# The second bias on the weights' queue, and the last expert's transposes ahead of its second product

## The chip, the cores and the metric

The kernel runs on one core of one Trainium2 chip. The metric is device microseconds of one launch, the median of the runs shown. A profile of one execution gives its span, from the first to the last instruction, and the busy time of each engine: TensorE (PE; its weight loads apart as PEld), VectorE (DVE), ScalarE (ACT), GpSimd (POOL) and the queue processor SyncE (SP). Transfers run on 16 DMA engines; they are issued here from SyncE's queue and from ScalarE's.

## The reference

One decoder layer on 256 tokens of width 1024, all in float32: a mixer (pooling, sparse attention and forgetting attention, merged by gates), a layer norm, then a mixture of experts and a second layer norm. The change lies in the mixture of experts. Cut to what matters:

```python
logits = xf @ router_w + router_b              # 256 tokens, 32 experts
top_v, top_i = lax.top_k(logits, 4)
gates = jax.nn.softmax(top_v, axis=-1)
# for every expert e and its tokens:
h = xblk @ w1[e] + b1[e]                       # 1024 -> 2048
gate, upv = jnp.split(h, 2, axis=-1)
gate = jnp.minimum(gate, 7.0); upv = jnp.clip(upv, -7.0, 7.0)
act = (upv + 1.0) * (gate * jax.nn.sigmoid(1.702 * gate))
y_e = act @ w2[e] + b2[e]                      # 1024 -> 1024
# y = sum over a token's experts of its gate times y_e
x = layer_norm(ALPHA * x + y, ln2_g, ln2_b)
```

`moe_b2`, the second bias, is a table of 32 experts by 1024 numbers, 128 KB. Its part of the result is the gates, 256 x 32, times this table.

## The kernel before

The mixer fills the first quarter of the span. The experts then run one after the other in a loop over `e` from 0 to 30, with expert 31 written out behind it. Each expert has 64 slots for tokens; where an expert has more, a second pass handles them (`overflow`, not taken here). An expert reads 12 MB of weights: four tiles of 2 MB for its first product (`First(e).load()`, a quarter of the 1024 rows each) and two for its second (`Second(e).load()`). Its steps are `gemm1` (64 slots by 1024 by 2048, into the two banks `h`), copies to `hs` by ScalarE and VectorE, `act` (transposes by TensorE, then bias, clamps, sigmoid and products on VectorE and ScalarE, into `a_main`), `gemm2` (into the bank `u`), and `scatter`, which spreads the slots over the tokens and adds them in the four banks `acc`. The second product of an expert runs within the pass of the next one; so pass `e` loads the first weights of `e` and then the second weights of `e - 1`.

All weights are issued by SyncE in one written order (`in_order`). They go into a ring of 11 places of 2 MB, by turns, so that a load can be issued when TensorE has read the load that stood 11 places earlier. Each transfer also signals on one of eight semaphores, which the order's rows name DMAHW0 to DMAHW7. They are given out in turn over the transfers of both queues, and a transfer is issued only when the one that had its semaphore before has landed.

The second bias was loaded in pass 2 by `load_biases`, with two transfers of 64 KB on ScalarE's queue, into `xg[2]`, a buffer for gathered tokens that is free for that time (the trace names it `rws`). In pass 3 `gated_biases` multiplies it with the gates into `acc`. Later, in pass 29, `norm_rows` puts the gain and the bias of the second layer norm as rows into a buffer `gb2` of its own pool.

Expert 31 is written out to the end. Its first product is taken with the first half of the columns finished first (`c` = 0), so that the activation of that half runs beside the product's other half. `act(..., c, DVE, parts=n)` handles half `c`: four transposes on TensorE, then the elementwise steps in `n` pieces. Its second product takes eight slices `j` of 128 rows: slices 0 to 3 need the activation's first half, 4 to 7 the second. Slices 0 to 5 run over all columns, 6 and 7 over one half of the columns at a time, so that the copy, the last `scatter` and the norm's sums of the first half start early. Its weights are loaded by `Last().load()`: slices 0 to 3 as 2 MB, slices 4 and 5 as 1 MB, slices 6 and 7 as two column halves of 512 KB.

Instructions issued through `PE`, `DVE`, `ACT` or `GPS` keep the order in which they are written; their line in the profile is line 48, the helper's.

Of the kernel before, what the change touches and what calls it, by code (L numbers as in the profile page):

```python
# [9 lines left out]
F32 = mybir.dt.float32  # L10
# [11 lines left out]
E = 32  # L22
# [29 lines left out]
def hybrid(ctx: ExitStack, tc: tile.TileContext, A, out, dbg=None):  # L52
    nc = tc.nc
    PE, DVE, ACT = Pinned(tc, nc.tensor), Pinned(tc, nc.vector), Pinned(tc, nc.scalar)
    GPS = Pinned(tc, nc.gpsimd)
    A = {n: a[0] for n, a in A.items()}
# [61 lines left out]
    b1T = consts.tile([128, 16, E], F32, name="b1T")  # L118
# [28 lines left out]
    def mm_tile(cols=256):  # L147
        return ps.tile([128, 512], F32, name="mm", bufs=3)[:, :cols]
# [17 lines left out]
    rows = mp.tile([128, 128], F32, name="rows")  # L166
# [96 lines left out]
    for t in range(2):  # L263
        for h in range(2):
            warm0(WARM_X[t * 2 + h])
            p = mm_tile(512)
# [3 lines left out]
            r = (slice(None), kq[h], slice(t * 128, (t + 1) * 128))  # L270
# [18 lines left out]
    def fm(w, c0, parts=None, pe=None, p=None, copy=nc.vector.tensor_copy):  # L289

        hi, lo = parts or hi_lo(8)
        if not parts:
            split(hi, lo, w[:, :, c0:c0 + 128], copy)
        if p is None:
            p = mm_tile(256)
        if pe:
            for n, (a, b) in enumerate(((hi, xh), (hi, xl), (lo, xh))):
                for k in range(8):
                    pe.matmul(p, a[:, k], b[:, k], start=(n == k == 0), stop=(n == 2 and k == 7))
        else:  # L300
            for k in range(8):
                mm3(p, (hi[:, k], lo[:, k]), (xh[:, k], xl[:, k]), k == 0, k == 7)
        return p
# [34 lines left out]
    for i in range(2):  # L338
        p = cmp_p[i]
# [24 lines left out]
    for br in range(2):  # L364
        p = fm(None, 0, kd_parts[br])
# [15 lines left out]
    p = mm_tile(256)[:32, :]  # L381
# [8 lines left out]
    p = mm_tile(64)  # L390
# [26 lines left out]
    for c in range(2):  # L417
        w = win((512 + 256 * c, 768 + 256 * c))
        for i in range(2):
            p = fm(w, i * 128)  # L420
            nc.scalar.activation(qn[:, 2 * c + i, :], p, AF.Identity, bias=col(R_A + 4 + 2 * c + i), scale=1.0)

    p = mm_tile(256)
# [461 lines left out]
    def slots(src, ts, dve=nc.vector):  # L885

        n = src.shape[-1]
        sh = [128, ts.stop - ts.start, n, SLOTS]
        return dve.tensor_tensor(S[:, ts, :n], src.unsqueeze(3).to_broadcast(sh),
                                 iota_s[:, None, None, :].to_broadcast(sh), op=OP.is_equal).ins  # L890

    def row_set(v, j, n):

        return v[:, j // n * n * 128:(j // n + 1) * n * 128].rearrange("p (c r) -> p r c", r=n)[:, j % n]
# [45 lines left out]
    norm_row_pool = ctx.enter_context(tc.tile_pool(name="norm_rows", bufs=1, side="right", reuse_waits="tile"))  # L940
    rings['x'] = xp
    r = turn[0] % len(order)
# [7 lines left out]
    def u_tile():  # L950
        return ps.tile([128, 512], F32, name="u", bufs=2)
# [4 lines left out]
    def h_tile(c):  # L956
        return ps.tile([128, 512], F32, name=f"h{c}")
# [36 lines left out]
    xg = [t2[:, b * 512:(b + 1) * 512].rearrange("p (k s) -> p k s", k=8) for b in range(2)]  # L994
# [41 lines left out]
    a_main = t2[:, 1024:1536].rearrange("p (j s) -> p j s", j=8)  # L1036
# [42 lines left out]
    def weigh(gsrc, x):  # L1079

        for t in range(2):
            nc.gpsimd.tensor_tensor(SG[:, t], S[:, t, x:x + 1].to_broadcast([128, 2, SLOTS]),  # L1082
                                    gsrc[:, t].unsqueeze(2).to_broadcast([128, 2, SLOTS]), op=OP.mult)

    def weigh_last(gsrc):

        for x in range(2):
            nc.gpsimd.tensor_tensor(S[:, :, x], S[:, :, 1], gsrc.to_broadcast([128, 2, SLOTS]), op=OP.mult)
# [9 lines left out]
    def gemm1(xg, w1):  # L1098

        hp = [h_tile(c) for c in range(2)]  # L1100
        for k in range(8):
            for c in range(2):
                for half in range(2):
                    PE.matmul(hp[c][half * 64:(half + 1) * 64], xg[:, k],
                              w1(k, half * 2 + c), start=(k == 0), stop=(k == 7), skip_group_check=True)
        nc.scalar.copy(hs[:, :512], hp[0])  # L1106
        nc.vector.tensor_copy(hs[:, 512:], hp[1])  # L1107
# [24 lines left out]
    def in_order(w, src):  # L1132
        return tc.keep_in_program_order(nc.sync.dma_start(w, src))

    def First(e):
        return Rows(w1v, e)

    def Second(e):
        return Rows(w2v, e)
# [64 lines left out]
    def act(*args, **kw):  # L1204
        for _ in act_steps(*args, **kw):
            pass
        return args[1]
# [14 lines left out]
                                 start=first, stop=False,  # L1222
                                 skip_group_check=True)

    def load_biases(dst):

        for h in range(2):
            ACT.dma_start(dst[h * E:(h + 1) * E], A['moe_b2'][:, h * 512:(h + 1) * 512])

    def gated_biases(b2r):  # L1230
        GT = lp.tile([128, T], F32, name="GT")
# [41 lines left out]

    def norm_rows():

        gb2 = norm_row_pool.tile([128, 2048], F32, name="gb2").rearrange("p (r c) -> p r c", c=128)
        for q in range(4):
            p = u_tile()
            for j in range(4):
                r = q * 4 + j  # L1280
                nc.tensor.matmul(p[:, j * 128:(j + 1) * 128], ident[:16, r:r + 1].to_broadcast([16, 128]), rows2,
                                 start=(j == 0), stop=(j == 3), skip_group_check=True)
            nc.scalar.copy(gb2[:, q * 4:(q + 1) * 4], p.rearrange("p (j c) -> p j c", j=4))
        return [gb2[:, i * 8:(i + 1) * 8].rearrange("p r c -> p (r c)") for i in range(2)]

    def gates(e):
        return G[:, :, e:e + 1]
# [5 lines left out]
    for e in range(E - 1):  # L1293
        buf, odd = e % 2, e % 2 == 1
        if e == E - 3:
            g2, b2 = norm_rows()
        w1 = First(e).load()
        if 0 < e < E - 2:
            w2 = Second(e - 1).load()
        if e:  # L1300
            weigh(gates(e), buf)
            if e == E - 2:
                weigh_last(gates(E - 1))
            if odd:
                slots(rk[:, :, e + 1:e + 3], slice(0, 2))
        gemm1(xg[e % 3], w1)
        if e == 0:
            p = u_tile()
            for c in range(4):
                PE.transpose(p[:, c * 128:(c + 1) * 128], row_set(b1r, c, 4), ident)  # L1310
            nc.scalar.copy(b1T.rearrange("p (q c) e -> p c q e", q=4), p.rearrange("p (c q e) -> p c q e", c=4, q=4))
            with tc.issue_after(last_pe), tc.issue_after(last_act), tc.issue_after(last_dve):
                acc[1] = [acc_tile(1, h) for h in range(2)]
                gates_and_counts()
            weigh(gates(0), 0)
            gT = turn_slots(0, u_tile())
            a = act(b1T[:, :, e], a_main)
        elif e < E - 2:
            if late:
                scatter(*late)  # L1320
                late = None
            a = xg[e % 3] if e == E - 3 else a_main
            steps = act_steps(b1T[:, :, e], a, banks=[u_tile(), h_tile(0)])
            next(steps)
            if e == 3:
                gated_biases(b2r)
            if odd:
                find(e + 1, 0, h_tile(1))
            else:
                gT = turn_slots(buf, h_tile(1))  # L1330
            gemm2(prev[0], w2)
            for _ in steps:
                pass
            if odd:
                gT = turn_slots(buf, h_tile(0))
                find(e + 1, 1, u_tile())
            late = prev[1], e == 1
            if e == 2:
                b2r = xg[2].rearrange("p k s -> p (k s)")
                load_biases(b2r)  # L1340
            if e == SUMS:
                scatter(*late)
                late = None
                residuals()
            if e == E - 3:

                scatter(*late)
                gemm2(a, Second(e).load())
        else:
            gT = turn_slots(buf, u_tile())  # L1350
            a = a_main
            steps = [act_steps(b1T[:, :, e], a, c, DVE) for c in range(2)]
            for c in range(2):
                next(steps[c])
            scatter(prev[1])
            gTn = turn_slots(1 - buf, h_tile(0), S)
            for c in range(2):
                for _ in steps[c]:
                    pass
            w2 = Second(e).load()  # L1360
            last = Last().load()
            gemm2(a, w2)
        prev = (a, gT)
# [9 lines left out]
    for c in range(2):  # L1373
        for k in (6, 7):
            last.first(banks, k, c)
        nc.scalar.copy(hs[:, c * 512:(c + 1) * 512], banks[c])
        if c:
            yp = h_tile(0)
            for j in (0, 1):
                last.second(yp, j, slice(0, 512))  # L1380
        act(b1T[:, :, E - 1], a_main, c, DVE, parts=2 - c)
    for j in range(2, 6):
        last.second(yp, j, slice(0, 512))

    def row_sums():
# [8 lines left out]
    for c in range(2):  # L1394
# [4 lines left out]
        for t in range(2):  # L1399
            for h in range(2):  # L1400
                r = slice(h * 64, (h + 1) * 64)
# [56 lines left out]
```

## Time and profile before

| | before |
|---|---|
| median of 3 runs (lowest, highest) | 1199.18 us (1198.42, 1199.37) |
| the profiled execution, its own time | 1200.99 us |
| its span | 1199.1 us |
| TensorE busy | 1128.9 us, 94% |
| VectorE busy | 347.7 us, 29% |
| ScalarE busy | 208.8 us, 17% |
| DMA, mean over the span | 375 GB/s |
| mean granted TensorE clock | 0.995 |

The span is cut in 40 slices of 30 us where the page shows rates over time. Busy shares are means over stages with different limits: the mixer (to about 260 us) has the DMA engines idle for part of the time, the experts have both TensorE and the DMA engines near full. Which of the two sets the end is not to be read from the shares but from the waits.

### The profile page before, as it was taken

The page shows a single profiled execution, that of the slowest core. Times are in us where ns is not written, and L with a number is a line of the kernel's source. Part 1 is how long each engine was busy: PE and PEld are TensorE (multiplying, and loading weights), DVE is VectorE, ACT ScalarE, POOL GpSimd, SP SyncE. Part 2 cuts the span into 40 slices and gives each one's busy share as a digit, 9 for nine tenths or more (in the row PEclk, how much of TensorE's full clock was granted, in tenths as well). Part 3 has the DMA queues.
Part 4 walks back from the last instruction along what each step waited for, and adds up shares of the span by engine and source line. Part 5 has one row for each costly group of instructions (what it writes and reads, how often), then busy time and mean ns, then how long its engine had stood idle before and what let it go on. Part 6 is the DMA issues. An engine that isn't in the chain of part 4 may idle for free.

```text
span 1199.1 us, 15184 instructions
## 1 busy us (share of the span) xinstructions
PE 1128.9 (94%) x6440; PEld 593.1 (49%) x6441; DVE 347.7 (29%) x709; ACT 208.8 (17%) x493; POOL 63.1 (5%) x106
## 2 busy tenths in 40 slices
PE   9999999999999999999989898989898989899994
PEld 8898889985434444343424242424242424244431
DVE  6579776473111211111111111111111111111114
ACT  5115444532100111010101010101010101011101
POOL 1010001311000000000000000000000000000000
PEclk9999999999999999999999999999999999999998
DMA  8994329779989999999999999999999999999993
GB/s 243 312 302 141 107 73 379 295 279 375 428 334 431 430 429 429 428 427 430 428 429 428 429 431 428 430 428 428 428 431 427 429 430 427 431 429 429 429 419 146
DMA packets 73042, 449.33 MB, mean 375 GB/s; under 512 B 8084, under 2 KB 41802, under 8 KB 48522
## 3 DMA queue, kind: packets, MB, share of 16 engines
q1 hardware_dynamic: 72366, 447.37, 91.1%
q8 instruction: 52, 0.85, 0.3%
q10 hardware_dynamic: 604, 0.94, 0.2%
q14 instruction: 20, 0.16, 0.0%
HBM read 447.25 MB, written 1.05 MB: 374 GB/s over the span
## 4 chain that ended last, share of the span: by engine, by line
DMA 52%; PE 45%; DVE 2%; ACT 0%; issue 0%; SPq 0%; ACTq 0%; DVEq 0%
DMA w<-in_moe_w_dram 51%; PE h L48 15%; PE u L48 8%; PE mm L94 4%; PE mm L95 4%; PE mm L96 4%; PE acc L48 2%; DMA w<-in_w_in_dram 1%; PE sc L648 1%; PE mm L48 1%; PE yps L693 1%; PE ptp L684 1%; PE sc L48 1%; DVE t L48 1%; PE ptp L48 0%; DMA x<-in_x_dram 0%
## 5 line engine op out<-in xcount | busy, mean ns | idle before, releaser
L48 PE MATMUL h<-w,t 128*64 128x512 f32 x1448 | 321.0, 593 | 36.9 <-DMA w<-in_moe_w_dram 34.6
L48 PEld LDWEIGHTS h<-w,t 128*64 128x64 f32 x1448 | 101.1, 137 | 246.3 <-issue 182.3
L48 PE MATMUL u<-w,t 128*64 128x512 f32 x960 | 213.3, 596 | 0.9 <-DMA w<-in_moe_w_dram 0.7
L1107 DVE COPY t<-h 128x512 f32<-128x512 f32 x31 | 21.5, 692 | 513.8 <-PE h L48 513.8
L48 PE MATMUL h<-w,rws 128*64 128x512 f32 x640 | 143.1, 600 | 11.6 <-DMA w<-in_moe_w_dram 10.1
L48 PEld LDWEIGHTS u<-w,t 128*64 128x64 f32 x960 | 66.4, 137 | 124.9 <-issue 118.1
L48 PEld LDWEIGHTS h<-w,rws 128*64 128x64 f32 x640 | 45.3, 138 | 104.5 <-issue 83.6
L94 PE MATMUL mm<-xhl,ws 128*128 128x256 f32 x336 | 96.8, 288 | 0.0
L96 PE MATMUL mm<-xhl,ws 128*128 128x256 f32 x336 | 95.1, 283 | 0.6 <-DVE ws L89 0.6
L95 PE MATMUL mm<-xhl,ws 128*128 128x256 f32 x336 | 95.0, 283 | 0.0
L1106 ACT COPY t<-h 128x512 f32<-128x512 f32 x31 | 18.2, 586 | 441.0 <-PE h L48 441.0
L89 DVE TENSOR_TENSOR ws<-w,ws 128x1024 fp32r<-128x1024 f32 (+1 forms) x64 | 73.3, 1149 | 11.8 <-ACT ws L88 10.8
L1082 POOL TENSOR_TENSOR ext<-ext,G 128x128 f32<-128x128 f32 x62 | 27.2, 458 | 818.2 <-PE h L48 799.5
L48 PE MATMUL acc<-t,ext 64*128 64x512 f32 (+1 forms) x264 | 63.9, 602 | 1.6 <-ACT t L1398 0.9
L94 PEld LDWEIGHTS mm<-xhl,ws 128*128 128x128 f32 x336 | 64.3, 191 | 1.0 <-issue 0.8
L96 PEld LDWEIGHTS mm<-xhl,ws 128*128 128x128 f32 x336 | 64.3, 191 | 0.8 <-DVE ws L89 0.8
L95 PEld LDWEIGHTS mm<-xhl,ws 128*128 128x128 f32 x336 | 64.4, 192 | 0.0
L1202 DVE SCALAR_TENSOR_TENSOR t<-t 128x512 f32<-128x512 f32 x29 | 20.1, 692 | 149.5 <-PE u L48 149.5
L1215 ACT COPY t<-u 128x512 f32<-128x512 f32 x31 | 18.2, 586 | 176.8 <-PE u L48 176.8
L48 PEld LDWEIGHTS acc<-t,ext 64*128 64x128 f32 x264 | 22.7, 186 | 41.1 <-issue 27.6
L1198 ACT ACTIVATE t<-t 128x512 f32<-128x512 f32 (+2 forms) x35 | 20.7, 593 | 94.6 <-DVE t L1197 84.7
L88 DVE CAST ws<-w 128x1024 fp32r<-128x1024 f32 (+1 forms) x47 | 29.4, 635 | 26.3 <-PE mm L96 13.7
(339 smaller groups left out, 1092.8 us busy)
## 6 DMA issues: line engine op xcount, KB each, us to landing
w<-in_moe_w_dram SPq DMA_DIRECT2D x190, 2048.0 KB
w<-in_w_in_dram SPq DMA_DIRECT2D x22, 1024.0 KB
w<-in_w_up_dram SPq DMA_DIRECT2D x6, 1024.0 KB
w<-in_cmp_w_dram SPq DMA_DIRECT2D x4, 1024.0 KB
w<-in_w_o_dram SPq DMA_DIRECT2D x4, 1024.0 KB
w<-in_w_in_dram SPq DMA_DIRECT2D x6, 512.0 KB
w<-in_moe_w_dram SPq DMA_DIRECT2D x6, 512.0 KB
w<-in_moe_w_dram SPq DMA_DIRECT2D x1, 1024.0 KB
```

Source lines behind the costliest of these rows:

```text
L48: return lambda *a, **k: self.tc.keep_in_program_order(f(*a, **k))
L88: copy(hi, src)
L89: return sub.tensor_tensor(lo, src, hi.bitcast(F32), op=OP.subtract).ins
L94: pe.matmul(p, ah, bh, start=first, stop=False, **kw)
L95: pe.matmul(p, ah, bl, start=False, stop=False, **kw)
L96: pe.matmul(p, al, bh, start=False, stop=last, **kw)
L1082: nc.gpsimd.tensor_tensor(SG[:, t], S[:, t, x:x + 1].to_broadcast([128, 2, SLOTS]), gsrc[:, t].unsqueeze(2).to_broadcast([128, 2, SLOTS]), ...
L1106: nc.scalar.copy(hs[:, :512], hp[0])
L1107: nc.vector.tensor_copy(hs[:, 512:], hp[1])
L1198: nc.scalar.activation(sg[i], gate[i], AF.Sigmoid, scale=1.702)
L1202: vec.scalar_tensor_tensor(a[:, js], up[i], 1.0, sg[i], op0=OP.add, op1=OP.mult)
L1215: nc.scalar.copy(ys, yp)
```

## The change

The second bias now has a buffer in the pool of the norm's rows: `b2r` and `gb2` share one place by their tag, first one and then the other. Its two transfers are issued by SyncE, in the written order of the weights, right behind expert 2's first weights, and no longer by ScalarE at the end of pass 2. In expert 31 the second half is activated ahead of the second product's first slices (before, slices 0 and 1 stood ahead of it), and it is activated in two pieces as the first half is.

```diff
-    def load_biases(dst):
+    def load_biases():
+        dst = norm_row_pool.tile([128, 2048], F32, name="b2r", tag="rows")[:2 * E, :512]
         for h in range(2):
-            ACT.dma_start(dst[h * E:(h + 1) * E], A['moe_b2'][:, h * 512:(h + 1) * 512])
+            in_order(dst[h * E:(h + 1) * E], A['moe_b2'][:, h * 512:(h + 1) * 512])
+        return dst
...
-        gb2 = norm_row_pool.tile([128, 2048], F32, name="gb2").rearrange("p (r c) -> p r c", c=128)
+        gb2 = norm_row_pool.tile([128, 2048], F32, name="gb2", tag="rows").rearrange("p (r c) -> p r c", c=128)
...
         w1 = First(e).load()
+        if e == 2:
+            b2r = load_biases()
         if 0 < e < E - 2:
             w2 = Second(e - 1).load()
...
             late = prev[1], e == 1
-            if e == 2:
-                b2r = xg[2].rearrange("p k s -> p (k s)")
-                load_biases(b2r)
...
         nc.scalar.copy(hs[:, c * 512:(c + 1) * 512], banks[c])
-        if c:
-            yp = h_tile(0)
-            for j in (0, 1):
-                last.second(yp, j, slice(0, 512))
-        act(b1T[:, :, E - 1], a_main, c, DVE, parts=2 - c)
-    for j in range(2, 6):
+        act(b1T[:, :, E - 1], a_main, c, DVE, parts=2)
+    yp = h_tile(0)
+    for j in range(6):
         last.second(yp, j, slice(0, 512))
```

The order on SyncE, before, from the last quarter of expert 2's first weights (w_3604) to the third quarter of expert 4's (w_3824). w_3609 and w_3610 are expert 1's second weights, w_3696 to w_3699 expert 3's first, w_3704 and w_3705 expert 2's second, w_3822 the first quarter of expert 4's first weights. DMAHW is the semaphore of an earlier transfer that a row waits for.

```order
L1133 DMA w_3604<-in_moe_w1_dram 128x4096 [waits DMAHW4_49,PE_49]
L1133 DMA w_3609<-in_moe_w2_dram 128x4096 [waits DMAHW5_49,PE_49]
L1133 DMA w_3610<-in_moe_w2_dram 128x4096 [waits DMAHW6_49,PE_49]
L1133 DMA w_3696<-in_moe_w1_dram 128x4096 [waits DMAHW0_49,PE_49]
L1133 DMA w_3697<-in_moe_w1_dram 128x4096 [waits DMAHW2_49,PE_49]
L1133 DMA w_3698<-in_moe_w1_dram 128x4096 [waits DMAHW3_49,PE_49]
L1133 DMA w_3699<-in_moe_w1_dram 128x4096 [waits DMAHW7_49,DMAHW4_49,PE_49]
L1133 DMA w_3704<-in_moe_w2_dram 128x4096 [waits DMAHW5_49,PE_49]
L1133 DMA w_3705<-in_moe_w2_dram 128x4096 [waits DMAHW6_49,DMAHW1_49,PE_49]
L1133 DMA w_3822<-in_moe_w1_dram 128x4096 [waits DMAHW7_49,PE_49]
L1133 DMA w_3823<-in_moe_w1_dram 128x4096 [waits DMAHW0_49,PE_49]
L1133 DMA w_3824<-in_moe_w1_dram 128x4096 [waits DMAHW1_49,PE_49]
```

The same place on SyncE in the change, from the same load of expert 2 to the first of expert 4, here w_3823; the weights behind the bias have other numbers (expert 2's second weights are w_3705 and w_3706).

```order
L1133 DMA w_3604<-in_moe_w1_dram 128x4096 [waits DMAHW4_49,PE_49]
L1133 DMA b2r_3609<-in_moe_b2_dram 32x512 [waits DMAHW5_49]
L1133 DMA b2r_3609<-in_moe_b2_dram 32x512 [waits DMAHW6_49]
L1133 DMA w_3612<-in_moe_w2_dram 128x4096 [waits DMAHW7_49,PE_49]
L1133 DMA w_3613<-in_moe_w2_dram 128x4096 [waits DMAHW0_49,PE_49]
L1133 DMA w_3697<-in_moe_w1_dram 128x4096 [waits DMAHW1_49,PE_49]
L1133 DMA w_3698<-in_moe_w1_dram 128x4096 [waits DMAHW2_49,PE_49]
L1133 DMA w_3699<-in_moe_w1_dram 128x4096 [waits DMAHW3_49,PE_49]
L1133 DMA w_3700<-in_moe_w1_dram 128x4096 [waits DMAHW4_49,PE_49]
L1133 DMA w_3705<-in_moe_w2_dram 128x4096 [waits DMAHW5_49,PE_49]
L1133 DMA w_3706<-in_moe_w2_dram 128x4096 [waits DMAHW6_49,PE_49]
L1133 DMA w_3823<-in_moe_w1_dram 128x4096 [waits DMAHW7_49,PE_49]
```

The bias transfers moved into this queue, ahead of expert 1's second weights. Before, ScalarE's two transfers had semaphores 7 and 1 (SyncE's rows skip them behind w_3610 and w_3696), so that w_3822 and w_3824 wait for them; in the change they have 5 and 6, and expert 2's second weights wait for them.

The order on TensorE in expert 31, before. `h_6716` is the bank of the first product's second half, `u` the transposes of the activation, `h_6771` the bank of the second product.

```order
L48 MATMUL h_6716<-w,t_3247 64x512 [waits DMAHW0_49]
L48 MATMUL h_6716<-w,t_3247 64x512 [waits DMAHW1_49]
L48 MATMUL h_6716<-w,t_3247 64x512 x2
L48 MATMUL h_6771<-w,t_3247 64x512 [waits DMAHW2_49,DVE_49,PE_49]
L48 MATMUL h_6771<-w,t_3247 64x512 x3
L48 MATMUL u<-ident,t_3248 128x128 [waits Activation_49]
L48 MATMUL u<-ident,t_3248 128x128 x3
L48 MATMUL h_6771<-w,t_3247 64x512 [waits DVE_49]
L48 MATMUL h_6771<-w,t_3247 64x512 x3
L48 MATMUL h_6771<-w,t_3247 64x512 [waits DMAHW3_49,DVE_49]
L48 MATMUL h_6771<-w,t_3247 64x512 x3
L48 MATMUL h_6771<-w,t_3247 64x256 [waits DMAHW4_49]
```

The same place in the change, where the banks are `h_6717` and `h_6788`.

```order
L48 MATMUL h_6717<-w,t_3247 64x512 [waits DMAHW0_49]
L48 MATMUL h_6717<-w,t_3247 64x512 [waits DMAHW1_49]
L48 MATMUL h_6717<-w,t_3247 64x512 x2
L48 MATMUL u<-ident,t_3248 128x128 [waits Activation_49]
L48 MATMUL u<-ident,t_3248 128x128 x3
L48 MATMUL h_6788<-w,t_3247 64x512 [waits DMAHW2_49,DVE_49,PE_49]
L48 MATMUL h_6788<-w,t_3247 64x512 x3
L48 MATMUL h_6788<-w,t_3247 64x512 [waits DVE_49]
L48 MATMUL h_6788<-w,t_3247 64x512 x3
L48 MATMUL h_6788<-w,t_3247 64x512 [waits DMAHW3_49,DVE_49]
L48 MATMUL h_6788<-w,t_3247 64x512 x3
L48 MATMUL h_6788<-w,t_3247 64x256 [waits DMAHW4_49,DVE_49]
```

The four transposes moved ahead of slices 0 and 1, the first rows of the second product, which wait for weights (DMAHW2).

## Rows read from the trace of the kernel before

**Rows 1.** The page: TensorE busy in tenths, and GB/s, in 40 slices.

```profile
PE   9999999999999999999989898989898989899994
...
GB/s 243 312 302 141 107 73 379 295 279 375 428 334 431 430 429 429 428 427 430 428 429 428 429 431 428 430 428 428 428 431 427 429 430 427 431 429 429 429 419 146
```

**Rows 2.** The chain that ended last: start us, us, what.

```profile
538.27 12.83 PE h L48 x59
551.09 40.22 DMA w<-in_moe_w_dram
...
1154.00 21.79 DMA w<-in_moe_w_dram
```

**Rows 3.** Busy time by stretch: us, engines, PEclk, DMA share, GB/s.

```profile
285.00:336.00 51.00, 50.25 (x254) 20.79 (x252) 9.63 (x18) 7.40 (x14) 1.77 (x4) 1.00 1.01 431
...
336.00:345.00 9.00, 9.00 (x48) 3.74 (x46) 3.08 (x6) 1.00 (x2) 0.76 (x2) 1.00 0.39 113
...
337.00:338.00 1.00, 1.00 (x10) 1.00 (x9) 0.21 (x1) 0.00 (x0) 0.00 (x0) 1.00 0.15 66
...
338.00:345.00 7.00, 7.00 (x36) 2.55 (x37) 2.87 (x6) 1.00 (x2) 0.76 (x2) 1.00 0.39 96
...
341.00:342.00 1.00, 1.00 (x8) 0.42 (x6) 0.43 (x1) 0.00 (x0) 0.00 (x0) 1.00 0.64 125
...
345.00:1166.00 821.00, 772.09 (x3778) 307.40 (x3776) 121.39 (x215) 80.26 (x176) 24.62 (x56) 1.00 1.01 429
```

**Rows 4.** SyncE's waits (us, times, longest), and issues in order of time.

```profile
SPq L1133 <- DMA rws<-in_moe_b_dram: 16.7, 1, 16.7
...
340.10 0.80 ACTq L48 DMA_DIRECT2D rws<-in_moe_b_dram  x2
...
341.99 2.16 SPq L1133 DMA_DIRECT2D w<-in_moe_w_dram  x4
```

**Rows 5.** Expert 2's first product in the chain, and SyncE's issues around it.

```profile
321.27 13.88 PE h L48 x64
...
319.06 0.33 SPq L1133 DMA_DIRECT2D w<-in_moe_w_dram  x1
...
324.90 17.42 SPq L1133 DMA_DIRECT2D w<-in_moe_w_dram  x2
...
345.51 26.01 SPq L1133 DMA_DIRECT2D w<-in_moe_w_dram  x6
```

**Rows 6.** TensorE's waits from 551 to 1166 us: us in total, times, longest.

```profile
PE h L48 <- DMA w<-in_moe_w_dram: 43.0, 39, 1.3
```

**Rows 7.** Expert 31 in order of time: start us, us, instruction [idle before <-releaser].

```profile
1165.57 5.37 PE L48 MATMUL h<-w,t 128*64 128x512 f32 x24 [0.60 <-DMA w<-in_moe_w_dram]
...
1172.41 0.69 DVE L48 TENSOR_TENSOR t<-u,b1T 128x512 f32<-128x512 f32 x1 [21.99 <-PE u L48]
...
1174.29 0.59 ACT L1376 COPY t<-h 128x512 f32<-128x512 f32 x1 [0.30 <-PE h L48]
...
1174.68 0.29 DVE L48 SCALAR_TENSOR_TENSOR t<-t 128x128 f32<-128x128 f32 x1
1175.93 1.94 PE L48 MATMUL h<-w,t 128*64 128x512 f32 x8 [1.69 <-DMA w<-in_moe_w_dram]
1177.80 0.75 PE L48 MATMUL u<-ident,t 128*128 128x128 f32 x4
...
1178.58 0.69 DVE L48 TENSOR_TENSOR t<-u,b1T 128x512 f32<-128x512 f32 x1 [3.61 <-PE u L48]
...
1181.10 2.83 PE h L48 x16
...
1183.95 0.37 ACT L1398 COPY t<-h 128x256 f32<-128x256 f32 x1 [3.82 <-PE h L48]
```

**Rows 8.** DMA by stretch near the end, and the page's issues of 512 KB.

```profile
1177.00:1180.00 3.00, 3.00 (x17) 1.04 (x12) 1.19 (x3) 0.29 (x1) 0.00 (x0) 1.00 0.45 161
...
w<-in_moe_w_dram SPq DMA_DIRECT2D x6, 512.0 KB
```

## The prediction

> **What bounds the kernel now.** I read the views in this order: the page for what is busy in which slice, the chain that ended last, the waits of the queue that issues the weights, then short stretches around the one place where the stream of weights stops, and last the rows of the final expert. The page shows two things that seem to bound: TensorE is over nine tenths busy in most slices, and the DMA engines carry 427 to 431 GB/s from the slice that begins at 360 us nearly to the end [rows 1]. One slice among them, 330 to 360 us, has only 334 GB/s. The chain decides between the two: from 551 us on it is expert weights in steps of about 40 us (the first stands in the rows), and the last step ends at 1175.79 us, where the last expert's second product begins [rows 2]. So after 551 us the end is set by when the weights land. Before 551 us the chain is TensorE; whether a DMA gap there costs anything has to be worked out, and I come to it below.
>
> The gap is at 338 us. Between 285 and 336 us the engines carry 431 GB/s, between 338 and 345 us 96 GB/s, and from 345 us to 1166 us a mean of 429 GB/s [rows 3]. What stopped them is the issuing queue: SyncE waited once for 16.7 us, for a bias transfer that ScalarE issues [rows 4]. ScalarE issued its two bias transfers at 340.10 us, SyncE its next load at 341.99 us, and then four loads within 2.16 us, as loads whose places had been free for a while do [rows 4]. The order of the program says why: the first load of expert 4 waits for the semaphore that the first bias transfer uses, though it has nothing else to do with it.
>
> **The change, part by part.** *The bias on SyncE.* ScalarE loses two issues, 0.80 us of its queue [rows 4], which nothing waits for. What counts is that the load of w_3822 no longer stands behind them. Its place comes free when TensorE has read the second quarter of expert 2's first weights: that product runs from 321.27 us for 13.88 us [rows 5], so its quarters end every 3.47 us: 324.7, 328.2, 331.7, 335.2 us. The load issued at 324.90 us fits the first of these; the next three were 14, 10 and 7 us late. The engines had work until about 337 us, so with these three issued on time the stream doesn't stop.
>
> How much is the stop worth? For the mean engine: 336 to 345 us moved 113 x 9 = 1017 KB, which at 429 GB/s is 2.37 us, so 6.63 us were lost [rows 3]. A transfer lands when its slowest engine is done, and a few engines (share 0.15) worked until 338 us; counted from there, 96 x 7 = 672 KB or 1.57 us, and 5.43 us were lost. I take 6.0 between them.
>
> The bias itself now lies in the stream. Its 131 KB were moved in the gap and count above as useful (0.3 us at 429 GB/s); they held the engines for a share of 0.64 over 1.00 us [rows 3]. So the extra price of the small pieces is 0 to 0.34 us; I take 0.2, since that row is of the very transfers.
>
> Does the earlier stream stay ahead of TensorE? A load is 2.097 MB, 4.89 us at 429 GB/s. With no gap the first load of expert 4 starts near 337.4 us and the n-th behind it at 337.4 + 4.89 n. Its place was free at 328.2 us, a margin of 9 us. After the gap six more issues lie between 345.51 us and 371.2 us [rows 5]; the last of them is n = 9, would start at 381.4 us, a margin of 10 us. Later the margin grows: TensorE reaches expert 10's first product at 538.27 us, eight experts after 321.27 us [rows 2, 5], 27.1 us for each, and the six loads of an expert take 29.3 us. So nothing eats the gain in the first part, and in the second TensorE idles behind the loads: 43.0 us in 39 waits between 551 and 1166 us [rows 6], of which the change leaves some 37.
>
> The new wait: the two bias issues stand in SyncE's queue right behind expert 2's last quarter, and the loads of w_3705 and w_3706 then wait for the bias semaphores. Those two took their turn near 319.06 us and 324.90 us [rows 5]. Eight loads of 4.89 us lie between the bias and the drained queue at 337 us, so the bias lands near 298 us: 21 us of cover. Its reader, in expert 3, comes after expert 2's first product, which ends at 335 us. Writing the norm's rows over the bias comes at expert 29 and waits for nothing. First part: 6.0 - 0.2 = **5.8 us**, bounds 5.1 and 6.6.
>
> *The transposes of the last expert.* ScalarE had copied the second half of the hidden rows by 1174.29 + 0.59 = 1174.88 us. The four transposes stood behind the matmuls of slices 0 and 1, which waited for weights until 1175.93 us, so they ran at 1177.80 us; VectorE and ScalarE worked on the activation from 1178.58 us; at 1181.10 us TensorE could go on with slices 4 and 5, and at 1183.95 us ScalarE copied the first half of the result [rows 7]. In the new order the transposes (0.75 us) run from about 1174.9 us, inside the wait for weights, and end before 1175.93 us. The activation in two pieces took 1172.41 to 1174.97 us for the first half, 2.56 us [rows 7]; in one piece it took 2.52 us from 1178.58 to 1181.10 us. It would end near 1178.3 us, beside the matmuls of slices 0 to 3. So from 1175.93 us TensorE does all its slices without a stop: 0 to 3 are 16 records, and 24 such records take 5.37 us in the row at 1165.57 us, so 3.4 to 3.6 us; 4, 5 and the first half of 6 and 7 take the 2.83 us of the row at 1181.10 us. That gives 6.25 to 6.45 us to the copy where there were 8.02 us: 1.6 to 1.8 us, I take **1.7**. The price of the two pieces, 0.04 us, is hidden under slices 0 to 3; without that cover it would be paid in full.
>
> It would be less if the last weights were late. From 1177 to 1180 us a share of 0.45 moves 161 GB/s, 358 GB/s at full share; the last two pieces are 512 KB each, 1.5 us, and the one before them, for slices 4 and 5, is 1 MB, 2.9 us [rows 8]. Back from 1180.1 us the data end at 1180.1, 1178.6 and 1177.1 us, and those of slices 0 to 3 at 1174.2 us, which were used 1.7 us after that. With 1.7 us on each, slices 4 and 5 are there at 1178.8 us and wanted at 1179.4 us, the first half of 6 and 7 at 1180.3 us and wanted at 1181.3 us, the other half at 1181.8 us and wanted a microsecond after ScalarE's copy at 1182.3 us. All are covered, the first by 0.6 us, and landing and use move together.
>
> **The sum.** 5.8 + 1.7 = 7.5 us. The profiled execution took 1200.99 us for a span of 1199.1 us, so its like would be 1193.5 us. The median of the three timed runs is 1199.18 us, so I predict **1191.7 us**. A measurement here tells 0.2% (2.4 us) from no change.
>
> **Rivals.** *Stream only* (0.11): TensorE is in order, and the transposes now stand ahead of the matmuls and wait for ScalarE's copy; were that copy later than the weights, the 1.7 us would shrink to nothing: 1193.4 us. Against it stands 1.05 us between the copy's end and the weights [rows 7].
>
> *Small transfers that the stream does not hide* (0.07): from the issue at 340.10 us to SyncE's release at 341.99 us the pair took 1.9 us [rows 4]. If the queue stops that long for each, 3.8 us go: 6.0 - 3.8 + 1.7 = 3.9, 1195.3 us. Against it: those 1.9 us are a latency seen in an empty queue, and loads that follow are already issued. The Trainium skill (DMA: Bandwidth & Descriptors, section Anatomy of one DMA) gives each DMA a fixed cost of about 2.0 us, for the gpsimd path. By it the sum would be, as an estimate, 6.0 - 4.0 + 1.7 = 3.7 us. The row of the pair agrees on the latency; no row shows that it stops a full queue.
>
> *The gap costs nothing* (0.06): the chain names TensorE until 551 us, so a stop at 338 us is not on it. Then only 1.7 us come: 1197.5 us. Against it: the chain takes the last releaser; the load that starts its step at 551 us was released by TensorE but lands 40 us later, behind a queue that has not stopped since 345 us [rows 2, 3]. The Trainium skill (the same page, section Issuing engines are not separate DMA queues) says that issuing from several engines only saves the sequencer's issue time. By that rule alone the move would be worth at most ScalarE's 0.80 us. The trace disagrees on this kernel: the 16.7 us wait is that of a queue for another queue's transfer.
>
> *Slower* (0.04): the bias lands late and holds SyncE at w_3705. The queue then runs dry from near 327 us; the time is above before's once the bias lands later than 327 + 7.5 = 334.7 us, and each microsecond past that costs one. At 339 us it would be 1203 us. That needs 36 us more than I estimate.
>
> **Chances and range.** Both parts as summed: 0.72. Faster by over 0.2%: 0.72 + 0.11 + 0.07 = 0.90; within 0.2%: 0.06; slower: 0.04. The low end is 6.6 + 1.8 = 8.4 us and half of the runs' spread (0.5 us) below: 1190.3, put at 1190.2. The high end takes in the stream alone with its low bound, 1199.18 - 5.1 = 1194.1 us, and a little of the next case: 1194.6.
>
> **What would show it.** Right: no wait for the bias in SyncE's queue; loads issued every 3.4 us through 328 to 335 us; about 430 GB/s from 336 to 345 us; the last expert's matmuls from the landing of its second weights to ScalarE's copy in 6.2 to 6.5 us, and the transposes before them. Wrong: a new stop of the stream between 319 and 380 us, or a pause before slices 4 and 5 or 6 and 7 that ends on a DMA.

## The result, and the profile after

The changed kernel takes 1191.53 us (median of 4 runs, 1190.87 to 1192.26) against 1199.28 us (4 runs); the ratio is 0.9935, 95% interval 0.9918 to 0.9952. That is 7.75 us where 7.5 were forecast.

The profiled spans are 10.0 us apart (1199.1 and 1189.1 us), more than the times. The rest lies ahead of anything that was changed: in the profile after, the mixer's last product (tile `sc`, 36 matmuls) starts in the chain at 256.51 us where it started at 258.64 us before, 2.13 us sooner, and the change edits nothing in the mixer. That start differs between executions of one kernel: a later profile of the changed kernel, on another chip, has it at 259.89 us. So I count within the experts, from the start of expert 0's first product to the first matmul of expert 31's second product ("the stream"), and from there to ScalarE's copy ("the tail"). The chain that ended last gives the starts (start us, us, what). Before, the second is at 1175.93 us [rows 7] and the first is

```profile
277.74 13.88 PE h L48 x64
```

After, the chain reads:

```profile
275.61 13.88 PE h L48 x64
...
1145.02 22.41 DMA w<-in_moe_w_dram
...
1167.56 6.25 PE h L48 x32
...
1173.83 0.38 ACT t L1396
```

The stream went from 898.19 us to 891.95 us, 6.24 us less; the tail from 8.02 us [rows 7] to 6.27 us, 1.75 us less; together 7.99 us. The forecast had 5.8 and 1.7.

The stop is gone. Busy time by stretch, after (the stretch and its length in us; busy us of PE, PEld, DVE, ACT and POOL, each with its number of instructions; PEclk, the granted TensorE clock as a share of the full one; the DMA engines' busy share; GB/s):

```profile
285.00:305.00 20.00, 19.36 (x98) 7.46 (x96) 4.74 (x10) 3.46 (x5) 0.76 (x2) 1.00 1.00 416
305.00:336.00 31.00, 30.89 (x163) 13.94 (x160) 5.23 (x9) 3.94 (x9) 1.01 (x2) 1.00 1.01 430
336.00:345.00 9.00, 9.00 (x45) 3.12 (x45) 3.43 (x7) 1.59 (x3) 0.76 (x2) 1.00 1.02 433
345.00:1158.00 813.00, 769.04 (x3770) 307.11 (x3768) 120.62 (x214) 79.60 (x175) 24.57 (x56) 1.00 1.01 429
```

Where 113 GB/s stood from 336 to 345 us [rows 3] there are 433. From 285 to 305 us the rate is 416 at a full share, 15 below what it was before (431): the two bias transfers pass there, as the short stretches show.

```profile
293.00:296.00 3.00, 3.00 (x18) 1.00 (x16) 1.50 (x4) 1.69 (x2) 0.00 (x0) 1.00 0.91 387
296.00:299.00 3.00, 3.00 (x18) 1.00 (x16) 1.39 (x2) 0.22 (x1) 0.00 (x0) 1.00 1.04 378
```

SyncE's issues after, in order of time, show the bias and the loads that were held before:

```profile
286.48 0.89 SPq L1133 DMA_DIRECT2D b2r<-in_moe_b_dram  x2
...
322.77 17.51 SPq L1133 DMA_DIRECT2D w<-in_moe_w_dram  x5
```

The first four of the five loads go out at 322.77, 326.20, 329.63 and 333.07 us, one every 3.43 us, with the quarters of expert 2's first product; before, one load waited 16.7 us there [rows 4]. No bias stands in SyncE's waits any more, and TensorE's waits for weights between 551 and 1158 us are 37.4 us in 34 times, as forecast (43.0 to 1166 us before [rows 6]):

```profile
PE h L48 <- DMA w<-in_moe_w_dram: 37.4, 34, 1.3
```

The last expert after, in order of time (start us, us, instruction [idle before <-releaser]):

```profile
1165.92 0.58 ACT L1377 COPY t<-h 128x512 f32<-128x512 f32 x1 [0.30 <-PE h L48]
...
1166.56 0.75 PE L48 MATMUL u<-ident,t 128*128 128x128 f32 x4 [0.69 <-ACT t L1377]
1167.34 0.69 DVE L48 TENSOR_TENSOR t<-u,b1T 128x512 f32<-128x512 f32 x1 [0.75 <-PE u L48]
1167.56 6.23 PE L48 MATMUL h<-w,t 128*64 128x512 f32 x32 [0.26 <-DMA w<-in_moe_w_dram]
...
1169.61 0.29 DVE L48 SCALAR_TENSOR_TENSOR t<-t 128x128 f32<-128x128 f32 x1
1173.83 0.37 ACT L1396 COPY t<-h 128x256 f32<-128x256 f32 x1 [4.92 <-PE h L48]
```

The transposes run inside the wait for weights, the activation ends at 1169.90 us beside the first slices, and TensorE goes through all its slices in one row of 32 records.

### The profile page after: what moved, and what is told of

Its sections match the earlier page's. It is cut to its first block, busy times and chain, and to the rows that moved or that the text cites. A ratio compares the mean times of both kernels' runs of the same rounds, so it can differ in the third digit from the quotient of the medians.

```text
span 1189.1 us, 15189 instructions
## 1 busy us (share of the span) xinstructions
PE 1125.0 (95%) x6440; PEld 591.9 (50%) x6441; DVE 347.8 (29%) x713; ACT 208.8 (18%) x494; POOL 64.4 (5%) x106
## 3 DMA queue, kind: packets, MB, share of 16 engines
HBM read 447.25 MB, written 1.05 MB: 377 GB/s over the span
## 4 chain that ended last, share of the span: by engine, by line
DMA 53%; PE 43%; DVE 2%; ACT 1%; SPq 1%; issue 0%; ACTq 0%; DVEq 0%
DMA w<-in_moe_w_dram 51%; PE h L48 15%; PE u L48 8%; PE mm L94 4%; PE mm L95 4%; PE mm L96 4%; PE acc L48 2%; DMA w<-in_w_in_dram 2%; PE sc L648 1%; PE yps L693 1%; PE ptp L684 1%; PE sc L48 1%; PE mm L48 1%; DVE t L48 0%; DMA x<-in_x_dram 0%; PE ptp L96 0%
## 5 line engine op out<-in xcount | busy, mean ns | idle before, releaser
L1106 ACT COPY t<-h 128x512 f32<-128x512 f32 x31 | 18.1, 585 | 434.0 <-PE h L48 434.0
```

## The experiments

The theory: the stop is SyncE standing in order behind a transfer of another queue whose semaphore it takes over; it costs as much as the loads already issued don't cover, and all of that is saved at the end. The rivals are named with each run.

**Each part alone.** With the last expert as before:

```diff
-        act(b1T[:, :, E - 1], a_main, c, DVE, parts=2)
-    yp = h_tile(0)
-    for j in range(6):
+        if c:
+            yp = h_tile(0)
+            for j in (0, 1):
+                last.second(yp, j, slice(0, 512))
+        act(b1T[:, :, E - 1], a_main, c, DVE, parts=2 - c)
+    for j in range(2, 6):
         last.second(yp, j, slice(0, 512))
```

> The bias on SyncE alone, the last expert as before. Theory (SyncE no longer stands behind ScalarE's transfer, and the stop of the stream is earned in full): 5.8 us of the measured 7.8 come from here, so about 1193.3 us against 1199.3, with no stop between 336 and 345 us and 8.0 us from the last weights to ScalarE's copy. Rival (the stop costs nothing because the chain before 551 us is TensorE): 1199 us, unchanged, with the stream's head start gone again by 551 us.

Measured 1193.36 us against 1199.72 us, ratio 0.9948 (0.9934 to 0.9962): 6.4 us. In its trace the stream is 892.28 us, 5.91 us less than before, the tail 8.02 us as before, and the stop is gone:

```profile
336.00:345.00 9.00, 9.00 (x45) 3.23 (x46) 3.65 (x7) 1.59 (x3) 0.76 (x2) 1.00 1.01 430
```

The reverse, the new last expert with the bias as before:

> The last expert's new order alone, the bias on ScalarE as before. Theory: 1.7 us, so about 1197.6 us; the stop at 338 us is still there, and from the last weights to the copy it takes 6.3 us instead of 8.0. Rival (the tail is worth the whole change and the stop nothing): 1191.5 us.

Measured 1197.75 us, ratio 0.9983 (0.9974 to 0.9992): 2.0 us in the times, and in the trace a tail of 6.27 us and a stream of 898.16 us, as before. The stop at 338 us costs in full, though the chain names TensorE there.

**Queue or place.** The bias at the new place in the program, but issued by ScalarE:

```diff
-            in_order(dst[h * E:(h + 1) * E], A['moe_b2'][:, h * 512:(h + 1) * 512])
+            ACT.dma_start(dst[h * E:(h + 1) * E], A['moe_b2'][:, h * 512:(h + 1) * 512])
```

> The changed kernel, but the two bias transfers issued by ScalarE at the new place in the program, the start of pass 2. Theory (a load stands behind the transfer whose semaphore it takes over, and ScalarE comes to it only when TensorE does): ScalarE gets there near 322 us, expert 3's third quarter, whose place is free near 308 us, is held until 324 us, the queue runs dry at about 317 us, so a stop of 7 to 8 us, earlier than before's: 1198 to 1199 us. Rival (the bias was only issued too late in the program): no stop, 1191.5 us.

Measured 1200.04 us, ratio 1.0003 (0.9994 to 1.0012): with the new last expert in it, it is no faster than before. Its stream is 900.35 us, 2.2 us longer than before's. SyncE's wait, and the stretches (columns as above):

```profile
SPq L1133 <- DMA b2r<-in_moe_b_dram: 19.2, 1, 19.2
```

```profile
312.00:316.00 4.00, 4.00 (x22) 1.34 (x20) 0.00 (x0) 0.00 (x0) 0.00 (x0) 1.00 0.94 401
316.00:321.00 5.00, 5.00 (x32) 2.90 (x30) 0.69 (x1) 1.51 (x4) 1.01 (x2) 1.00 0.03 13
321.00:326.00 5.00, 5.00 (x26) 1.68 (x24) 0.00 (x0) 0.00 (x0) 0.00 (x0) 1.00 0.48 105
```

The stop moved to 316 us with the load that now stands behind the bias: by the count of SyncE's issues it is the 19th of the experts' weights, expert 3's third quarter, where before it was the 23rd. It is longer too, and longer than I expected: against 430 GB/s these three stretches lost 0.3 + 4.8 + 3.8 = 8.9 us. Written earlier, the transfer on ScalarE's queue does more harm, not less. ScalarE issues it at 319.95 us, 20 us sooner than before, but the load that stands behind it could go 21 us sooner (its wait begins near 304.2 us, before's near 325.3 us), and the wait ends 3.4 us after ScalarE's issue where before it ended 1.9 us after; why that took longer the run doesn't show. The other way round, the old place with SyncE's queue:

```diff
         w1 = First(e).load()
-        if e == 2:
-            b2r = load_biases()
...
             late = prev[1], e == 1
+            if e == 2:
+                b2r = load_biases()
```

> The changed kernel, but the bias loaded at the old place in the program, the end of pass 2, still by SyncE. Theory (the issuing queue decides, not the place): the transfers stand behind expert 1's second weights and land before 310 us; no stop, 1191.5 us within 0.5. Rival (the earlier place earned the time): the stop comes back in part, 1194 to 1198 us.

Measured 1192.35 us, ratio 0.9934 (0.9920 to 0.9947): 0.35 us above the range I expected, and without a stop. Its stream is 892.31 us, 6 us shorter than before's. So the queue decides, not the place in the program. Nor does the place in memory. The old place and ScalarE's queue, into the norm rows' buffer (the edits of the two runs just shown, together):

> The changed kernel with the bias in the norm rows' place but issued by ScalarE at the end of pass 2, as before. Theory (the place in memory plays no part): the stop is back as it was, about 1197.8 us. Rival (the buffer of gathered tokens, which the old load shared, held something up): 1191.8 us.

Measured 1198.33 us, ratio 0.9990 (0.9981 to 0.9999). The stop is there, and the stream of 898.12 us is before's:

```profile
336.00:345.00 9.00, 9.00 (x45) 3.19 (x45) 3.60 (x7) 1.59 (x3) 0.76 (x2) 1.00 0.50 166
```

**What covers a held load.** On another chip the changed kernel was run once more, for comparison:

> The changed kernel once more, on the same chip as the next three, as what they are compared with: 1191.5 to 1192.5 us, 0.9935 of before.

Measured 1191.82 us, ratio 0.9930 (0.9917 to 0.9944). Then the same pair once more on ScalarE's queue, late in the stream:

```diff
             late = prev[1], e == 1
+            if e == 20:
+                for h in range(2):
+                    ACT.dma_start(b2r[h * E:(h + 1) * E], A['moe_b2'][:, h * 512:(h + 1) * 512])
```

> The changed kernel with two bias transfers more, into the same place, issued by ScalarE at the end of pass 20 as before's were at the end of pass 2 (what they bring is not read). Theory (a held load costs only when the loads already issued run out): the first load of expert 22 is held for some 7 us, but six loads of 4.9 us are then in the queue, so no stop; 0.3 us more than the changed kernel, at most 0.7. Rival (each pair on ScalarE's queue costs the stream some 6 us): 6 us more, about 1198 us.

Measured 1192.87 us, ratio 0.9937 (0.9923 to 0.9950), 1.05 us above the changed kernel, where I expected 0.3 and at most 0.7. By the times alone that is inside the spread (1191.31 to 1194.48 us here, 1191.23 to 1194.25 us there); by the streams it is 893.15 us against 892.21 us, 0.9 us. SyncE was held, and the engines did not stop; its wait, and the stretches of that time:

```profile
SPq L1133 <- DMA b2r<-in_moe_b_dram: 5.7, 2, 4.8
```

```profile
780.00:800.00 20.00, 16.74 (x76) 5.25 (x74) 2.52 (x6) 1.21 (x2) 0.15 (x1) 1.00 1.00 428
800.00:820.00 20.00, 18.78 (x104) 9.22 (x102) 4.12 (x7) 2.81 (x7) 1.01 (x2) 1.00 1.01 429
820.00:840.00 20.00, 18.85 (x90) 6.88 (x88) 2.77 (x6) 1.41 (x4) 0.76 (x2) 1.00 1.01 429
840.00:860.00 20.00, 15.90 (x74) 4.96 (x70) 1.69 (x3) 1.21 (x2) 0.00 (x0) 1.00 1.01 415
```

The rate falls to 415 GB/s at a full share in the stretch where ScalarE issues the pair (840.1 us). That is what a pair costs in the runs on small transfers below, so I take the microsecond for the pair's own price; this run alone doesn't show it. With `e == 4` in place of `e == 20`:

> The same two transfers more, but at the end of pass 4. Theory: ScalarE issues them near 394 us, the first load of expert 6 is held to 395.5 us; by the count of loads the queue runs out at about 394 us, so a stop of 1 to 3 us and as much more time than the changed kernel: 1193 to 1195 us. Rival (each pair costs some 6 us wherever it stands): about 1198 us.

Measured 1195.80 us, ratio 0.9960 (0.9947 to 0.9974): 4.0 us above the changed kernel. SyncE was held 18.1 us and the engines did run out:

```profile
394.00:401.00 7.00, 7.00 (x34) 2.30 (x32) 1.80 (x4) 1.22 (x2) 0.00 (x0) 1.00 0.60 190
```

Against 430 GB/s that stretch lost 3.9 us, 0.9 above the top of what I expected: SyncE issued again from 397.52 us, but the rate is 2 GB/s from 397 to 398 us and comes to 393 GB/s only from 401 us on. The three doses side by side: held 16.6 to 16.8 us in pass 2, some 6.9 us of stream (below); 18.1 us in pass 4, 3.9 us; 5.7 us in pass 20, none. The length of the wait on the issuing queue alone doesn't give the price. In pass 2 the engines still had work for some 12 us after the last load that SyncE had issued (324.90 us to near 337 us), in pass 4 for some 16 us (379.00 us to near 395 us), so the longer wait cost less there. In pass 20 the wait was also the shortest.

**The price of small transfers.** Fourteen more of 64 KB on SyncE, a pair a pass (`b2rows` is the whole buffer, which `load_biases` then returns too):

```diff
+        if 10 <= e < 17:
+            i = e - 9
+            for h in range(2):
+                in_order(b2rows[(i // 4 * 2 + h) * E:(i // 4 * 2 + h + 1) * E, i % 4 * 512:(i % 4 + 1) * 512],
+                         A['moe_b2'][:, h * 512:(h + 1) * 512])
```

> The changed kernel with 14 transfers of 64 KB more on SyncE, a pair in each of the passes 10 to 16, into parts of the norm rows' place that nothing reads. Theory (small transfers cost the stream their share of the engines): 0.3 to 0.64 us a pair, so 2.1 to 4.5 us more than the changed kernel. Rival (a fixed 1.9 to 2.0 us each that the stream doesn't hide): 27 us more.

Measured 1200.92 us, ratio 1.0008 (0.9999 to 1.0017), 9.1 us above the changed kernel: 0.65 us each, 1.3 us a pair. The streams are 9.4 us apart (901.60 us and 892.21 us). That is neither the theory's number nor the rival's. The stretches with a pair, and one without (540 to 550 us):

```profile
530.00:540.00 10.00, 10.00 (x56) 4.56 (x54) 0.99 (x2) 1.71 (x5) 1.01 (x2) 1.00 1.01 377
540.00:550.00 10.00, 10.00 (x50) 3.37 (x48) 0.00 (x0) 0.00 (x0) 0.00 (x0) 1.00 1.00 426
560.00:570.00 10.00, 10.00 (x48) 3.31 (x46) 0.69 (x1) 0.58 (x1) 0.00 (x0) 1.00 1.00 383
```

The engines stay busy and move 10 to 12% less in those ten microseconds; the pair takes their time, not the queue's. The Trainium skill (DMA: Bandwidth & Descriptors, section Anatomy of one DMA) has about 2.0 us fixed for each transfer on the gpsimd path; for fourteen that would be, as an estimate, 28 us if none were hidden, and the run, whose transfers SyncE issues, shows a third of it.

**The pair left out.** The bias transfers replaced by a fill with zeros, so that the second bias is missing from the result:

```diff
-        for h in range(2):
-            in_order(dst[h * E:(h + 1) * E], A['moe_b2'][:, h * 512:(h + 1) * 512])
+        nc.vector.memset(dst, 0.0)
         return dst
```

> The changed kernel without the two bias transfers: the table is set to zero instead, so the second bias is left out of the result. It gives the price of the pair in the stream. By the forecast's term, 0.5 us with the bytes: 1191.3 us. By the fourteen small transfers (9.1 us for seven pairs, 1.3 us a pair): 1190.5 us.

Measured 1192.99 us, ratio 0.9943 (0.9929 to 0.9957), more than either expectation, so by its time the run says nothing on the price: the fill landed in VectorE's steps between the mixer and the experts. In the chain:

```profile
266.10 0.48 DVE b2r L1228
...
278.75 13.88 PE h L48 x64
...
1170.05 6.25 PE h L48 x32
```

Expert 0 begins 20.9 us after the mixer's product on `ptp` ends, 1.8 us later than in the change. The fill itself is 0.48 us of that; what made the rest isn't shown. Counted from expert 0's first product, the stream is 891.30 us. In five runs with the pair in SyncE's queue in pass 2 (the change twice, and three variants) it is 891.95 to 892.31 us, so the pair costs 0.65 to 1.0 us at that place.

**A better place.** The pair a pass earlier, where the engines stop anyhow because no place in the ring is free (in the change their share is 0.08 from 272 to 274 us, while SyncE waits for TensorE):

```diff
         if 0 < e < E - 2:
             w2 = Second(e - 1).load()
+        if e == 1:
+            b2r = load_biases()
```

> The changed kernel with the bias loaded by SyncE already in pass 1, behind expert 0's second weights, where the engines stop for want of free places near 275 us anyway. If the pair's price is time of full engines, it is free there: 0.5 to 1.3 us less than the changed kernel, 1190.5 to 1191.3 us. Rival (the pair costs the same anywhere, or holds back the next load): 1191.8 us or a little more.

Measured 1190.31 us (1190.16 to 1190.78), ratio 0.9922 (0.9908 to 0.9935). That is 0.2 us below the range I expected, and it is the fastest of all: its five runs lie below the lowest of the nine runs of the change (1190.87) and below all five of the next run, on the same chip (1191.32 to 1192.88). The intervals of the two ratios overlap. The stream is 891.23 us, and the pair's price is gone:

```profile
275.97 13.88 PE h L48 x64
...
1167.20 6.25 PE h L48 x32
```

**Two pieces or one.**

```diff
-        act(b1T[:, :, E - 1], a_main, c, DVE, parts=2)
+        act(b1T[:, :, E - 1], a_main, c, DVE, parts=2 - c)
```

> The changed kernel with the second half's activation in one piece, as before. Theory (the elementwise steps run beside slices 0 to 3): no change, 1191.8 us within 0.5, and from the last weights to the copy 6.25 us as with two pieces. Rival (the two pieces bring part of the 1.7 us): up to 0.5 us slower, with a pause before slices 4 to 7.

Measured 1191.73 us, ratio 0.9935 (0.9921 to 0.9948), the change's own; the tail is 1174.92 - 1168.65 = 6.27 us, to the hundredth what it is with two pieces.

## Why the prediction was right, point by point

*The stop and its cause* were right: the wait on the bias is gone, the rate from 336 to 345 us is 433 GB/s, and only the runs with the pair on ScalarE's queue early in the stream have a stop.

*That the stop is earned in full although the chain names TensorE until 551 us* was right: each part alone gave its share, 6.4 and 2.0 us in the times against 5.8 and 1.7 (5.91 and 1.75 us in the traces).

*The size of the stop* (6.0 us, from 5.4 by the slowest engines to 6.6 by the mean engine) was low. With the pair free of charge the stream is 891.2 to 891.3 us; with the stop it is 898.1 to 898.2 us (before, and the two runs with ScalarE's queue at the old place): 6.9 us. In the forecast's terms, where the pair's bytes (0.3 us) counted as useful, that is 6.6: the mean engine's value. The deduction for the slowest engines was wrong here.

*The price of the pair* (0.3 us of bytes and 0.2 extra) was low too, by 0.15 to 0.8 us: it is 0.65 to 1.3 us by the four ways of measuring it (the pair left out, moved, issued once more, and seven pairs more). Its bound, a share of 0.64 over a microsecond, was read where the engines had nothing else to do. The two errors work against each other. In the five runs with the pair on SyncE's queue in pass 2 the stream is 5.8 to 6.2 us shorter than with the stop; that the sum of 5.8 us came so close is in part luck.

*The cover of the new wait* (21 us) held: in no run does SyncE wait for a pair that it issued itself. The forecast had the bias landing near 298 us, and the rate dips between 293 and 299 us; the first load that needs one of its semaphores goes out at 316.93 us, some 18 us later. *The margin to TensorE* held: in the change there is no rate under 429 GB/s in a long stretch from 305 to 1158 us.

*The tail* was right: 1.75 us against 1.7, the transposes inside the wait, the last weights landed in time, and the two pieces hidden under the first slices, which the run with one piece confirms.

*A slip in the rival "slower"*: 327 + 7.5 is 334.5 us, not 334.7. Nothing else rests on it.

The runs that differ only in the queue differ by 6.0 us (old place) and by 8.2 to 8.5 us (new place, against the two medians of the change). The Trainium skill (DMA: Bandwidth & Descriptors, section Issuing engines are not separate DMA queues) says that issuing from several engines saves only the time of issuing; taken alone, that would have made the move worth ScalarE's 0.80 us of issuing [rows 4] at most, and these runs disagree. They do not speak against the page's other statement there, that the transfers share the same 16 engines; the cost lies in the order in which semaphores are handed from one queue to the other.

## What to carry to other kernels

Look for a long wait of the weights' queue on a transfer that its loads take no data from, and read the rates of the DMA engines around it: only the part in which the engines run out of loads costs. A small load that belongs in a prefetch stream should be issued by the queue of that stream, ahead of need, and best where the stream stops anyway; on the queue of an engine that keeps step with the computation, writing it earlier can make it worse, as it did here. And a stop of the stream early in a program can be worth all its time even where the chain that ended last names another engine there.

## What the runs showed of the hardware that was not expected

A 64 KB transfer of 2 KB rows into 32 partitions, in the middle of a full stream of 2 MB loads, takes 0.65 us of it (14 of them, 9.1 us), although its bytes are 0.15 us at the stream's rate; the busy share of the engines stays at 1.00 to 1.01 meanwhile. What in the engines takes that time, these runs don't show.
